# A two-layer decoder step on one core: larger interleaving steps in the attention, moved key turns, and another order at the switch to the output projection

## The chip, the cores and the metric

The kernel runs on one core of a Trainium2 chip. The metric is the device time of one execution in microseconds (us). The engines are TensorE (PE, with its weight loads as PEld), VectorE (DVE), ScalarE (ACT), GpSimd (POOL) and SyncE (SP), which issues most DMAs.

## The reference, cut to what matters

The program runs one inference step of a two-layer trunk over 1040 prompt rows (16 meta tokens and 1024 new ones) and over 8 sampled sequences of 8 new rows each. Layer 0 is a Mamba-2 mixer and a gated feed-forward. Layer 1, where the change lies, is a sliding-window attention (window 128, 16 query heads, 4 key heads of 64) and a second feed-forward:

```
q = rope((rmsnorm(h) * attn_g) @ w_q);  k, v as one shared pair from (rmsnorm(h) * kv_g)
s = q . k / 8                       # only 0 <= t - s < 128; the sampled rows also see 128 stored keys
m = max(max(s), sink[head]);  p = exp(s - m) / (sum(exp(s - m)) + exp(sink[head] - m))
h = h + (p @ v) @ w_o               # then h = h + ffn(h), and a final rmsnorm
```

All inputs are float32. A projection product is computed as three products of a high and a low part in fp32r (`mm3`: high x high, high x low, low x high). Scores, transposes and values are plain float32 products.

## The kernel before, in words

Before the stage of the change come the mixer, layer 0's feed-forward and the key and value projections (`qkv`, up to about 1793 us). Then three kinds of work are laid into one another by Python generators. Each `yield` ends a step, and `joined`/`mix` advance two generators at a given ratio. PE runs the matmuls in the order in which they were written (`in_order` over everything from `forced` on, L2331 and L2376). The order on the other engines is chosen by a planner that simulates the program, by readiness and priority.

The query projection (`queries`, called `qs`) makes 16 row blocks of 128 rows x 512 columns, eight steps each, a step being the three matmuls of one k (L73 to L75). Its result is scaled on ACT (L1963), rotated on POOL (L1778 to L1780) and turned by four transposes (L2005) inside the next block; the last block's turn stands at the end (L2023).

The prompt attention has 16 units (8 row blocks x 2 halves of the heads), class `PromptUnit`. `scores(0)` and `scores(1)` are four 64-row products each (L2073), added to a mask and reduced by DVE (L2079). `softmax` is one small and eight long exponentials on ACT (L2090, L2096), sums on DVE and two multiplications on POOL (L2099). `turn(0)` and `turn(1)` are six transposes each (L2112), copied by ACT (L2114) and, the middle part after the second, by DVE (L2119). `values` are 16 products (L2130, L2134), copied by ACT and DVE (L2137). In `prompt` the loop over x lays unit x's scores, unit x-1's softmax and unit x-2's turns and values together in five steps.

The sampled attention (`attend_sample`) has four steps for each of 8 sequences: turn the stored keys (L2160), scores (L2171, L2172) and softmax, turn the probabilities (L2185, L2186), values (L2196, L2197). SP loads the next sequence's stored keys and values, and writes 120 rows of them back, at the start of a sequence.

The three are laid together so: 24 query steps first; then 64 prompt steps (units up to x = 13) at 2 to 1 with 32 sampled steps; these 96 against the 104 query steps left. Accumulators are eight banks in four rings of two (L55): scores, turned, out (also used for the middle turn, L2107) and rows (projections).

At the switch the attention results so far are split into high and low parts (`split_copy`: ACT casts at L79, DVE subtracts at L80), all fifteen pieces at high priority (L2369). Five more attention steps run (`AHEAD`, L54), then the first half's output projection (`output_early`, 64 steps of six matmuls of 272 columns) is mixed with the remaining eleven attention steps at 4 to 5. Each projected tile is saved to DRAM by SP (L2233). Then `output_tile` projects the second half, eight tiles, each saved by SP (L2252, L1268), and layer 1's feed-forward follows.

Of the kernel before, what the change touches and what calls it, by code (L numbers as in the profile page):

```python
# [21 lines left out]
NS = 64  # L22
# [28 lines left out]
FIRST = 3  # L51
LEAD = 3
EARLY = 14
AHEAD = 5  # L54
PLACES = {"scores": ("S", 2), "turned": ("T", 2), "out": ("O", 2), "rows": ("P", 2)}  # L55

HALVES = (
# [981 lines left out]
        yield  # L1039


def mix(*args):

    for _ in joined(*args):
        pass


END = object()
# [161 lines left out]
class FeedForward:  # L1210
# [685 lines left out]
def qkv(tc, K, A, ap, fp, ps, O, I, pre):  # L1896


    nc = tc.nc
# [239 lines left out]

def attend_sample(tc, K, A, sp, ps, I, O, order):  # L2140

    nc = tc.nc
    state = []

    def load(b):
        ks, v = sp.get("kst"), sp.get("vst")
        nc.sync.dma_start(ks, I["state_k"][b].rearrange("l h d -> l (h d)"))
        nc.sync.dma_start(v, I["state_v"][b].rearrange("l h d -> l (h d)"))
        nc.sync.dma_start(O["k_s"][b, 0:120].rearrange("l h d -> l (h d)"), ks[8:])
        nc.sync.dma_start(O["v_s"][b, 0:120].rearrange("l h d -> l (h d)"), v[8:])  # L2150
        state.append((ks, v))

    load(order[0])
    for x, b in enumerate(order):
        ks, v = state.pop(0)
        if x < 7:
            load(order[x + 1])
        pk = ps.turned()
        for kv in range(NKV):
            nc.tensor.transpose(pk[:64, 128 * kv : 128 * kv + 128], ks[:, 64 * kv : 64 * kv + 64], K.ident)  # L2160
        kT = sp.get("kT", 64)
        nc.vector.tensor_copy(kT, pk[:64, :])
        q4 = sp.get("q4", 64).rearrange("p (h t) -> p h t", t=8)
        nc.gpsimd.tensor_copy(q4[:, :8], A.QS[:64, :, 8 * b : 8 * b + 8])
        nc.scalar.copy(q4[:, 8:], A.QS[64:, :, 8 * b : 8 * b + 8])
        yield
        pss = ps.scores()
        for kv in range(NKV):
            rows = slice(32 * kv, 32 * kv + 32)
            q = q4[:, 4 * kv : 4 * kv + 4].rearrange("p h t -> p (h t)")  # L2170
            nc.tensor.matmul(pss[rows, 0:128], q, kT[:, 128 * kv : 128 * kv + 128], start=True, stop=True, tile_position=(0, 32 * kv))  # L2171
            nc.tensor.matmul(pss[rows, 128:192], q, A.KS[:, kv, :], start=True, stop=True, tile_position=(0, 32 * kv))  # L2172
        P = sp.get("PD")
# [11 lines left out]
        nc.tensor.transpose(pt[:, 0:128], P[:, 0:128], K.ident)  # L2185
        nc.tensor.transpose(pt[:64, 128:256], P[:, 128:192], K.ident)  # L2186
        PT = sp.get("PTd")
        nc.vector.tensor_copy(PT[:, 0:128], pt[:, 0:128])
        nc.scalar.copy(PT[:64, 128:256], pt[:64, 128:256])
        yield  # L2190
        po = ps.turned()
        for kv in range(NKV):
            a, e = divmod(kv, 2)
            out = po[64 * e : 64 * e + 64, 32 * a : 32 * a + 32]
            vs = slice(64 * kv, 64 * kv + 64)
            nc.tensor.matmul(out, v[:, vs], PT[:, 32 * kv : 32 * kv + 32], start=True, stop=False)  # L2196
            nc.tensor.matmul(out, A.V[:NS, 0, vs], PT[:64, 128 + 32 * kv : 160 + 32 * kv], start=False, stop=True)  # L2197
        nc.scalar.copy(A.OS[:, :, 8 * b : 8 * b + 8], po[:, :64].rearrange("p (q t) -> p q t", t=8))
        yield


# [12 lines left out]
def output_early(nc, K, F, sqh, rows, oH, oL):  # L2214


    for m in range(KD):
# [5 lines left out]
        for c in range(2):  # L2223
            acc = rows()
            cs = slice(272 * c, 272 * c + 272)
            for k in range(KD):
                wH, wL = (t[:, 128 * (k % 4) : 128 * (k % 4) + 128] for t in w[k // 4])
                mm3(nc, acc[:, :272], wH, wL, oH[:, k, cs], oL[:, k, cs], k == 0, k == KD - 1)
                if k == KD - 1:
                    nc.vector.tensor_tensor(x[:, cs], x[:, cs], acc[:, :272], ALU.add)  # L2230
                    output_square(nc, K, F, sqh, x[:, cs], 0, m, 272 * c)
                    if c:
                        nc.sync.dma_start(F.saved[0][:, m], x)  # L2233
                if k % 2:
                    yield

# [18 lines left out]
def attention(tc, K, I, O, pre):  # L2255
# [6 lines left out]
    with ExitStack() as outer:  # L2262
        outer.enter_context(F.stack.pop_all())
        with ExitStack() as inner:
# [32 lines left out]
            with tp(name="qf", bufs=1) as fp:  # L2297
# [11 lines left out]
                def prompt(first, last, done=lambda u: None):  # L2309

                    n = len(units)
                    for x in range(first, last):
                        if x < n:
                            units[x].scores(0)
                            yield
                        if x >= 2:
                            units[x - 2].turn(0)
                            yield
                        if x < n:
                            units[x].scores(1)  # L2320
                            yield
                        if 0 <= x - 1 < n:
                            units[x - 1].softmax()
                        if x >= 2:
                            units[x - 2].turn(1)
                            yield
# [5 lines left out]
                for _ in range(8 * LEAD):  # L2332
# [28 lines left out]
            def split(u):  # L2361

                e, fs, o = u.i // 4, slice(4 * u.a, 4 * u.a + 4), 32 + 128 * (u.i % 4)
                split_copy(nc, OH[e][:, fs, o : o + 128], OL[e][:, fs, o : o + 128], u.O)

            with tc.high_priority(PRIO):
# [117 lines left out]
```

## Time and profile before

| | us |
|---|---|
| median of 3 runs | 2869.57 (2868.34 to 2872.6) |
| the profiled execution | 2869.85 |
| its span, first to last instruction | 2868.1 |
| PE busy | 2760.2 (96%) |
| DVE busy | 2022.5 (71%) |
| ACT busy | 1222.4 (43%) |
| POOL busy | 487.1 (17%) |

The span is what the profiler saw between the first and the last instruction; the execution's own time is 1.75 us longer. Busy shares are means over stages with different limits, so a stage is read by its own stretch. A busy PE means that a matmul is under way; at the lower of the clock's two levels (1.2 instead of 2.4 GHz) the same matmul is busy longer. The granted clock is given as a share of the higher level.

### The profile page before, as it was taken

To read this page: it belongs to the slowest core of one execution; us is meant where nothing else is said; L and a number is where in the kernel's file an instruction comes from. 1 tells how busy PE (TensorE), PEld (TensorE's weight loads), DVE (VectorE), ACT (ScalarE), POOL (GpSimd) and SP (SyncE) were. 2 spreads that over 40 slices of the span, in tenths; PEclk is the share of its full clock that TensorE was granted. 3 is DMA by queue.
4 is the path that set the end of the run, shared out by engine and by line. 5 is a ranking of instruction groups with operands and counts; after the bars stand their busy time and mean duration, and the time that the engine had idled before them with its cause. 6 is when DMAs were issued, how large, how long until landed. Compare 5 with 4: busy or idle time off the path is not lost. (4 is left out here: it accounts for less than half of the span.)

```text
span 2868.1 us, 51222 instructions
## 1 busy us (share of the span) xinstructions
PE 2760.2 (96%) x19990; PEld 2545.5 (89%) x19990; DVE 2022.5 (71%) x3633; ACT 1222.4 (43%) x2580; POOL 487.1 (17%) x692
## 2 busy tenths in 40 slices
PE   7999999899999899999999999998999999999998
PEld 7888989877888799999999997665998999999998
DVE  6779676647574698777768791555479777877786
ACT  4667554346442344333332243545434433433224
POOL 1455444314222100000000002332210000000000
PEclk9999999999999999999999999998999999999999
DMA  6776866565554434444468652001623443437664
GB/s 201 236 233 225 273 216 215 183 234 192 198 177 169 137 99 171 136 150 140 138 258 305 227 198 79 20 23 50 184 88 114 171 136 131 161 142 303 239 219 156
DMA packets 327009, 496.58 MB, mean 173 GB/s; under 512 B 24479, under 2 KB 222559, under 8 KB 325713
## 3 DMA queue, kind: packets, MB, share of 16 engines
q1 hardware_dynamic: 325614, 491.20, 50.5%
q8 instruction: 158, 2.59, 0.4%
q10 hardware_dynamic: 1152, 2.10, 0.2%
q14 instruction: 85, 0.70, 0.1%
HBM read 317.93 MB, written 175.30 MB: 172 GB/s over the span
## 5 line engine op out<-in xcount | busy, mean ns | idle before, releaser
L1149 ACT CAST wo<-ws 128x512 fp32r<-128x512 f32 x428 | 263.7, 620 | 546.1 <-PE wacc L1492 246.5
L1491 PE MATMUL dacc<-bo,wo 128*128 128x276 f32 (+1 forms) x1232 | 360.3, 292 | 10.3 <-DMA bo<-f_B 5.4
L1493 PE MATMUL dacc<-bo,wo 128*128 128x276 f32 (+1 forms) x1232 | 358.0, 291 | 0.0
L1492 PE MATMUL dacc<-bo,wo 128*128 128x276 f32 (+1 forms) x1232 | 357.9, 291 | 0.0
L1150 DVE TENSOR_TENSOR wo<-ws,wo 128x512 fp32r<-128x512 f32 x428 | 297.4, 698 | 69.0 <-ACT wo L1149 59.6
L73 PE MATMUL acc<-uH,wH 128*128 128x296 f32 (+1 forms) x840 | 276.5, 329 | 1.7 <-DVE th L762 1.6
L74 PE MATMUL acc<-uL,wH 128*128 128x296 f32 (+1 forms) x840 | 275.5, 328 | 0.0
L75 PE MATMUL acc<-uH,wL 128*128 128x296 f32 (+1 forms) x840 | 274.2, 326 | 0.9 <-DVE wL L156 0.9
L1491 PEld LDWEIGHTS dacc<-bo,wo 128*128 128x128 f32 x1232 | 234.4, 190 | 11.5 <-issue 10.9
L1492 PEld LDWEIGHTS dacc<-bo,wo 128*128 128x128 f32 x1232 | 234.4, 190 | 0.0
L1493 PEld LDWEIGHTS dacc<-bo,wo 128*128 128x128 f32 x1232 | 234.1, 190 | 0.0
L73 PEld LDWEIGHTS acc<-uH,wH 128*128 128x128 f32 x840 | 158.9, 189 | 16.7 <-issue 6.6
L75 PEld LDWEIGHTS acc<-uH,wL 128*128 128x128 f32 x840 | 158.8, 189 | 11.6 <-issue 2.3
L74 PEld LDWEIGHTS acc<-uL,wH 128*128 128x128 f32 x840 | 158.8, 189 | 10.6 <-issue 2.2
L585 DVE SCALAR_TENSOR_TENSOR cc<-raw,convw,cc 128x616 f32<-128x616 f32 (+1 forms) x144 | 134.3, 936 | 39.5 <-ACT cc L583 37.9
L1639 DVE TENSOR_TENSOR hN<-hN,dacc 128x544 f32<-128x544 f32 (+1 forms) x164 | 116.7, 720 | 27.9 <-PE dacc L1493 26.4
L73 PE MATMUL acc<-yH,wH 128*128 128x296 f32 (+1 forms) x360 | 122.3, 342 | 6.9 <-ACT yH L79 3.7
L2285 POOL MEMSET mask<- 128x64 f32 x1 | 0.2, 154 | 727.0 <-PE dacc L1493 727.0
L74 PE MATMUL acc<-yL,wH 128*128 128x296 f32 (+1 forms) x360 | 120.6, 336 | 0.1
L75 PE MATMUL acc<-yH,wL 128*128 128x296 f32 (+1 forms) x360 | 120.2, 335 | 0.0
L1491 PE MATMUL wacc<-N4H,wo 128*128 128x276 f32 (+1 forms) x352 | 102.7, 292 | 4.7 <-DVE hN L1504 2.4
L1149 ACT CAST wo<-sum 128x512 fp32r<-128x512 f32 x66 | 41.0, 622 | 154.3 <-PE wacc L1492 106.7
(594 smaller groups left out, 8615.3 us busy)
## 6 DMA issues: line engine op xcount, KB each, us to landing
kept<-wH SPq DMA_DIRECT2D x56, 512.0 KB
kept<-wL SPq DMA_DIRECT2D x56, 512.0 KB
ws<-ffn_w_gate SPq DMA_DIRECT2D x44, 512.0 KB
ws<-ffn_w_up SPq DMA_DIRECT2D x44, 512.0 KB
ws<-ffn_w_down SPq DMA_DIRECT2D x44, 512.0 KB
ws<-ssm_w_in SPq DMA_DIRECT2D x40, 512.0 KB
wH<-kept SPq DMA_DIRECT2D x38, 512.0 KB
wL<-kept SPq DMA_DIRECT2D x38, 512.0 KB
```

Source lines behind the costliest of these rows:

```text
L73: nc.tensor.matmul(out, wH, xH, start=start, stop=False)
L74: nc.tensor.matmul(out, wH, xL, start=False, stop=False)
L75: nc.tensor.matmul(out, wL, xH, start=False, stop=stop)
L585: nc.vector.scalar_tensor_tensor(o, raw[:, k : k + n], w(k), o, ALU.mult, ALU.add)
L1149: nc.scalar.copy(H, src)
L1150: (low or nc.vector).tensor_tensor(L, src, H.bitcast(F32), ALU.subtract)
L1491: nc.tensor.matmul(out, wH, xH, start=start, stop=False, skip_group_check=True)
L1492: nc.tensor.matmul(out, wH, xL, start=False, stop=False, skip_group_check=True)
L1493: nc.tensor.matmul(out, wL, xH, start=False, stop=stop, skip_group_check=True)
L1639: add = lambda d, s: nc.vector.tensor_tensor(d, d, s, ALU.add)
L2285: nc.gpsimd.memset(A.mask0[:, :NS], NEG)
```

## The change

In words: (1) A query step holds two k, six matmuls. (2) A prompt unit has three steps for five: turn(0) of unit x-2 with scores(0) of x; turn(1) of x-2 with scores(1) and the softmax of the same x; values of x-2. (3) `together` puts one sampled step directly behind each prompt step while there are any; the 40 pairs are mixed with the 52 query steps left. (4) The next sampled sequence's keys are turned between a sequence's scores and its turned probabilities; two sequences are loaded at the start, and x+2 after the values of x. (5) The sampled scores take their bank from the ring of `out` instead of `scores`. (6) The last block's queries are turned after two attention steps of the second part. (7) At the switch only the pieces that the first half's projection reads are split at high priority, in the order of need; five others follow at normal priority. (8) Two attention steps instead of five run ahead of the projection, and the mix is 2 to 5. (9) The single tiles of the projection are saved by DMAs from ACT instead of SP.

```diff
-AHEAD = 5
+AHEAD = 2
+def together(a, b):
+    for _ in a:
+        next(b, END)
+        yield
+    for _ in b:
+        pass
 # FeedForward.save
-        start = (self.nc.sync if self.layer or m is None else self.nc.scalar).dma_start
+        start = (self.nc.sync if m is None else self.nc.scalar).dma_start
 # qkv, queries
-                    yield
+                    if k % 2:
+                        yield
...
-        turned.pop(0)()
+        A.last_turn = turned.pop(0)
 # attend_sample: four functions, keys, scores, turn, values, of the same instructions
-        pss = ps.scores()
+        pss = ps.rest()
...
+    load(0)
+    load(1)
+    for x, b in enumerate(order):
+        if x == 0:
+            keys(b, S[x])
+            yield
+        scores(b, S[x])
+        yield
+        if x + 1 < len(order):
+            keys(order[x + 1], S[x + 1])
+            yield
+        turn(S[x])
+        yield
+        values(b, S[x])
+        load(x + 2)
         yield
 # output_early
-                        nc.sync.dma_start(F.saved[0][:, m], x)
+                        nc.scalar.dma_start(F.saved[0][:, m], x)
 # attention, prompt
                     for x in range(first, last):
+                        if x >= 2:
+                            units[x - 2].turn(0)
                         if x < n:
                             units[x].scores(0)
-                            yield
+                        yield
                         if x >= 2:
-                            units[x - 2].turn(0)
-                            yield
+                            units[x - 2].turn(1)
                         if x < n:
                             units[x].scores(1)
-                            yield
-                        if 0 <= x - 1 < n:
-                            units[x - 1].softmax()
+                            units[x].softmax()
+                        yield
                         if x >= 2:
-                            units[x - 2].turn(1)
-                            yield
                             units[x - 2].values()
                             done(units[x - 2])
                             yield
...
-                att = joined(prompt(0, EARLY), sample, 5 * EARLY - 6, 32)
-                mix(att, qs, 5 * EARLY - 6 + 32, 8 * (16 - LEAD))
+                att = together(prompt(0, EARLY), sample)
+                mix(att, qs, 3 * EARLY - 2, 4 * (16 - LEAD))
...
             with tc.high_priority(PRIO):
-                for e, o, a, b in ((0, 0, 40, 64), (0, 24, 32, 40), (1, 0, 0, 32)):
-                    split_copy(nc, OH[e][:, :, o : o + b - a], OL[e][:, :, o : o + b - a], A.OS[:, :, a:b])
-                for u in units[: EARLY - 2]:
-                    split(u)
+                split_sampled(0, 0, 40, 64)
+                split_sampled(0, 24, 32, 40)
+                for i in range(4):
+                    split(units[i])
+                    split(units[8 + i])
+            split_sampled(1, 0, 0, 32)
+            for i in range(4, 8):
+                split(units[i])
...
             for _ in range(AHEAD):
                 next(att)
-            mix(att, early, 4, 5)
+            A.last_turn()
+            mix(att, early, 2, 5)
```

## Rows read from the trace of the kernel before

**Rows 1.** Stretches of time: busy us of each engine (instructions), PE clock, DMA share, GB/s

```profile
1793.20:1985.20 192.00, 181.37 (x1231) 122.99 (x1229) 99.08 (x425) 94.65 (x359) 69.97 (x120) 1.00 0.11 31
1985.20:1988.10 2.90, 0.18 (x1) 0.00 (x0) 1.25 (x2) 2.62 (x8) 2.84 (x5) 1.00 0.01 3
1988.10:2008.60 20.50, 15.41 (x63) 9.73 (x64) 16.15 (x47) 12.72 (x34) 2.17 (x5) 0.50 0.17 48
2008.60:2067.70 59.10, 58.87 (x471) 54.51 (x470) 27.23 (x61) 26.13 (x64) 14.78 (x16) 1.00 0.61 175
2067.70:2119.30 51.60, 51.13 (x402) 50.41 (x401) 35.20 (x65) 17.39 (x32) 9.55 (x6) 1.00 0.54 161
2119.30:2180.00 60.70, 49.14 (x354) 47.14 (x353) 50.94 (x93) 25.07 (x44) 1.62 (x1) 0.94 0.12 36
```

**Rows 2.** Waits of PE, 1793.2 to 1985.2: us in total, times, longest

```profile
PE pO L2130 <- ACT work L2114: 4.9, 4, 1.6
PE pT L2185 <- POOL work L2182: 3.1, 4, 1.6
PE pO L2130 <- ACT work L2116: 2.3, 2, 1.4
```

**Rows 3.** PE in order of time (start, us): values that wait, and that don't

```profile
1966.51 0.65 PE L2130 MATMUL pO<-work,V 128*64 128x256 f32 x2
1968.08 1.08 PE L2130 MATMUL pO<-work,V 128*64 128x256 f32 x6 [0.92 <-ACT work L2114]
...
1969.68 0.50 PE L73 MATMUL pP<-rwH,uH 128*128 128x512 f32 x1
...
1982.82 1.08 PE L2130 MATMUL pO<-work,V 128*64 128x256 f32 x8
...
1984.42 0.50 PE L73 MATMUL pP<-rwH,uH 128*128 128x512 f32 x1
```

**Rows 4.** ACT in order of time at the first: exponentials, then the copy

```profile
1963.84 0.46 ACT L2096 ACTIVATE work<-work 128x192 f32<-128x192 f32 x1 [2.64 <-DVE work L2089]
...
1967.46 0.56 ACT L2114 COPY work<-pT 128x512 f32<-128x512 f32 x1
```

**Rows 5.** DVE by line, 1793.2 to 1985.2: busy us, mean ns, idle before

```profile
L2079 DVE CUSTOM_DVE_ANT_0 work<-pS,am_sb,sink 128x192 f32<-128x192 f32 (+1 forms) x104 | 37.6, 409 | 30.5 <-PE pS L2073 30.5
```

**Rows 6.** PE in order of time: scores, projection, transposes, projection

```profile
1976.54 0.92 PE L2073 MATMUL pS<-KT,QT 64*128 64x192 f32 x8
1977.39 0.50 PE L73 MATMUL pP<-rwH,uH 128*128 128x512 f32 x1
1977.73 0.39 PE L74 MATMUL pP<-rwL,uH 128*128 128x512 f32 x1
...
1978.20 0.27 PE L2112 MATMUL pT<-cmask_sb,work 128*128 128x128 f32 x1
...
1978.77 0.48 PE L73 MATMUL pP<-rwH,uH 128*128 128x512 f32 x1
```

**Rows 7.** Waits of PE, 1985.2 to 2068: us in total, times, longest

```profile
PE pT L2005 <- POOL qr L1780: 4.1, 1, 4.1
PE pO L2130 <- DVE work L2119: 3.3, 2, 3.1
```

**Rows 8.** POOL in order of time at the switch

```profile
1985.26 1.47 POOL L2099 TENSOR_TENSOR work<-work 128x768 f32<-128x768 f32 x1 [0.72 <-DVE work L2098]
...
1989.13 0.32 POOL L1780 TENSOR_TENSOR qr<-rt,rt 128x64 f32<-128x64 f32 x1
```

**Rows 9.** ACT in order of time at the switch: the casts of the splits

```profile
1987.94 6.34 ACT L79 CAST OH<-QT 128x512 fp32r<-128x512 f32 x12
```

**Rows 10.** SP's waits, 2030 to 2180; issues of line 1268 by ACT (ns)

```profile
SPq L1268 <- DVE hN L2250: 26.6, 7, 7.3
...
L1268 ACTq DMA_DIRECT2D res<-big x8: 326/326/338, 966.9 to 983.7; - x8
```

**Rows 11.** Waits of PE, 2068 to 2181

```profile
PE ps L1077 <- POOL tot L2211: 4.4, 1, 4.4
```

More of the change, by code (lines that the diff above doesn't have):

```diff
@@ L2142, in attend_sample @@
     nc = tc.nc
[L2143 to L2157, printed above, removed]
+    S = [Ctx() for _ in order]
@@ new lines, in load, with keys @@
+    def load(x):
+        if x >= len(order):
+            return
+        b, s = order[x], S[x]
+        s.ks, s.v = sp.get("kst"), sp.get("vst")
+        nc.sync.dma_start(s.ks, I["state_k"][b].rearrange("l h d -> l (h d)"))
+        nc.sync.dma_start(s.v, I["state_v"][b].rearrange("l h d -> l (h d)"))
+        nc.sync.dma_start(O["k_s"][b, 0:120].rearrange("l h d -> l (h d)"), s.ks[8:])
+        nc.sync.dma_start(O["v_s"][b, 0:120].rearrange("l h d -> l (h d)"), s.v[8:])
+    def keys(b, s):
@@ L2158, in attend_sample @@
         pk = ps.turned()
         for kv in range(NKV):
[L2160 to L2165, printed above, removed]
-        yield
-        pss = ps.scores()
+            nc.tensor.transpose(pk[:64, 128 * kv : 128 * kv + 128], s.ks[:, 64 * kv : 64 * kv + 64], K.ident)
@@ L2168, in attend_sample, with scores @@
+        s.kT = sp.get("kT", 64)
+        nc.vector.tensor_copy(s.kT, pk[:64, :])
+        s.q4 = sp.get("q4", 64).rearrange("p (h t) -> p h t", t=8)
+        nc.gpsimd.tensor_copy(s.q4[:, :8], A.QS[:64, :, 8 * b : 8 * b + 8])
+        nc.scalar.copy(s.q4[:, 8:], A.QS[64:, :, 8 * b : 8 * b + 8])
+    def scores(b, s):
+        pss = ps.rest()
         for kv in range(NKV):
             rows = slice(32 * kv, 32 * kv + 32)
-            q = q4[:, 4 * kv : 4 * kv + 4].rearrange("p h t -> p (h t)")
-            nc.tensor.matmul(pss[rows, 0:128], q, kT[:, 128 * kv : 128 * kv + 128], start=True, stop=True, tile_position=(0, 32 * kv))
+            q = s.q4[:, 4 * kv : 4 * kv + 4].rearrange("p h t -> p (h t)")
+            nc.tensor.matmul(pss[rows, 0:128], q, s.kT[:, 128 * kv : 128 * kv + 128], start=True, stop=True, tile_position=(0, 32 * kv))
@@ L2172, in attend_sample @@
             nc.tensor.matmul(pss[rows, 128:192], q, A.KS[:, kv, :], start=True, stop=True, tile_position=(0, 32 * kv))
-        P = sp.get("PD")
+        P = s.P = sp.get("PD")
         m, nm, es, sm = (sp.get(x) for x in ("dm", "dn", "de", "ds"))
@@ L2182, in attend_sample, with turn, values @@
         nc.gpsimd.tensor_scalar(P, P, sm, None, ALU.mult)
-        yield
+    def turn(s):
         pt = ps.turned()
[L2185 to L2189, printed above, removed]
-        yield
+        nc.tensor.transpose(pt[:, 0:128], s.P[:, 0:128], K.ident)
+        nc.tensor.transpose(pt[:64, 128:256], s.P[:, 128:192], K.ident)
+        s.PT = sp.get("PTd")
+        nc.vector.tensor_copy(s.PT[:, 0:128], pt[:, 0:128])
+        nc.scalar.copy(s.PT[:64, 128:256], pt[:64, 128:256])
+    def values(b, s):
         po = ps.turned()
@@ L2195, in attend_sample @@
             vs = slice(64 * kv, 64 * kv + 64)
-            nc.tensor.matmul(out, v[:, vs], PT[:, 32 * kv : 32 * kv + 32], start=True, stop=False)
-            nc.tensor.matmul(out, A.V[:NS, 0, vs], PT[:64, 128 + 32 * kv : 160 + 32 * kv], start=False, stop=True)
+            nc.tensor.matmul(out, s.v[:, vs], s.PT[:, 32 * kv : 32 * kv + 32], start=True, stop=False)
+            nc.tensor.matmul(out, A.V[:NS, 0, vs], s.PT[:64, 128 + 32 * kv : 160 + 32 * kv], start=False, stop=True)
         nc.scalar.copy(A.OS[:, :, 8 * b : 8 * b + 8], po[:, :64].rearrange("p (q t) -> p q t", t=8))
+    load(0)
[13 more added lines that the diff above has]
+        load(x + 2)
         yield
@@ L2312, in prompt @@
                     for x in range(first, last):
+                        if x >= 2:
+                            units[x - 2].turn(0)
                         if x < n:
                             units[x].scores(0)
-                            yield
+                        yield
                         if x >= 2:
-                            units[x - 2].turn(0)
-                            yield
+                            units[x - 2].turn(1)
                         if x < n:
                             units[x].scores(1)
-                            yield
-                        if 0 <= x - 1 < n:
-                            units[x - 1].softmax()
+                            units[x].softmax()
+                        yield
                         if x >= 2:
-                            units[x - 2].turn(1)
-                            yield
                             units[x - 2].values()
@@ L2331, in attention @@
                 forced = len(traced)
-                for _ in range(8 * LEAD):
+                for _ in range(4 * LEAD):
                     next(qs)
                 sample = attend_sample(tc, K, A, sp, ps, I, O, (4, 5, 6, 7, 0, 1, 2, 3))
-                att = joined(prompt(0, EARLY), sample, 5 * EARLY - 6, 32)
-                mix(att, qs, 5 * EARLY - 6 + 32, 8 * (16 - LEAD))
+                att = together(prompt(0, EARLY), sample)
+                mix(att, qs, 3 * EARLY - 2, 4 * (16 - LEAD))
             pre.stack.close()
@@ L2364, in split, with split_sampled @@
                 split_copy(nc, OH[e][:, fs, o : o + 128], OL[e][:, fs, o : o + 128], u.O)
+            def split_sampled(e, o, a, b):
+                split_copy(nc, OH[e][:, :, o : o + b - a], OL[e][:, :, o : o + b - a], A.OS[:, :, a:b])
             with tc.high_priority(PRIO):
-                for e, o, a, b in ((0, 0, 40, 64), (0, 24, 32, 40), (1, 0, 0, 32)):
-                    split_copy(nc, OH[e][:, :, o : o + b - a], OL[e][:, :, o : o + b - a], A.OS[:, :, a:b])
-                for u in units[: EARLY - 2]:
-                    split(u)
+                split_sampled(0, 0, 40, 64)
[6 more added lines that the diff above has]
+                split(units[i])
             early = output_early(nc, K, F, sqh, ps.rows, OH[0], OL[0])
```

## The prediction

> **What bounds the kernel now.** Read first the stages as stretches of time [rows 1]. The diff touches the fourth quarter only: the woven attention (1793.2 to 1985.2 us), the switch to the output projection (1985.2 to 2008.6), the first half's projection woven with the last attention (to 2067.7) and the second half's projection (to 2119.3). The reader is to see PE busy for 181.37 of 192.00 us, 15.6 of 23.4, 58.87 of 59.10 and 51.13 of 51.60 there, while no other engine passes 52% in the first, or 70% in any of them but the switch. PE sets the pace, so what it loses is what can be won: 10.6 us of idle in the weave, and the whole of the switch, where 20.5 us run at a granted clock of 0.50 (the 1.2 GHz level). After 2119.3 the stage that follows is DVE's (50.94 of 60.70 us); it starts when PE is done and is not shortened by the diff.
>
> Then read who PE waits for in the weave [rows 2]: the values of a prompt unit wait 4.9 + 2.3 us for ACT's copies of the turned probabilities, the sampled turn 3.1 us for POOL's multiplication: 10.3 us in ten waits. The values' wait costs more than the view lists. A values block that waits goes from 1966.51 to the next projection matmul at 1969.68, 3.17 us; one that doesn't takes 1984.42 - 1982.82 = 1.60 [rows 3]. That is 1.57 lost for 0.92 listed, 0.65 more, since two matmuls are started before the idle begins. Six times 0.65 is 3.9, so the weave loses 14.2 us. The reason stands on ACT [rows 4]: the eight exponentials of the next unit run from 1963.84 to 1967.46, 3.6 us, and the copy that the values need stands behind them.
>
> At the switch read PE's waits [rows 7], and the clock in rows 1. From 1985.2 to 2008.6 PE is busy 0.18 + 15.41 us; the 15.41 are at half clock, so they are 7.7 us of work at full clock. 23.4 - 7.9 = 15.5 us are lost there: 4.1 in the wait for the last rotated queries, 3.1 and 0.2 in the values', 7.7 in the clock, the rest in small gaps.
>
> **The change part by part.** The sum starts from the profiled execution: 2869.85 us, of which 2868.1 are span and 1.75 lie around it. The median of the runs shown is 2869.57, so nothing is corrected.
>
> *Larger steps, softmax earlier.* No matmul is added or removed. Between the second half's turn and the values there stood one or two projection steps of three matmuls; a matmul of 512 columns follows the last after 0.235 us (1977.73 to 1978.20 for two [rows 6]), so 0.7 or 1.4 us. Now there stand the second scores (0.85), a sampled piece, and one or two steps of six (1.4 or 2.8): at least 2.25 us, against a copy of 0.56 us [rows 4]. And the exponentials of that step can't begin before it, since they need four reductions of 0.41 us, 1.6 us, after scores that come behind the turn [rows 5]. The six waits of the values go: -11.1 us (7.2 + 3.9).
>
> *Keys between scores and turned probabilities.* A whole step with its projection matmuls now stands between a sampled sequence's scores and its turn, 4 us or so instead of 0.7 to 1.4. The waits were 3.1 us in four, 1.6 at most, so they go: -3.1. The loads: still 32 state transfers on SP; two sequences at the start, then each behind the values two sequences before it. SP waits for PE there as it did before, and what is queued behind it is the w_o tiles, which nothing needs before 1985. The new keys are wanted two steps, some 8 us, after their load is issued: no cost.
>
> *Sampled scores in the ring of two that holds the middle turn and the values.* Twice in eight their step falls directly behind a unit's values, whose first copy is on ACT, now behind that unit's exponentials. Exponentials end 1.6 + 3.6 = 5.2 us after the second scores, the copy (0.4, a half of the 0.56 row and its overhead) at 5.6; the values end 2.65 + 1.60 = 4.25 after them at the earliest. So 1.3 us each, 2.6 in all. Bounds: 0 if the copy goes first, 2 x (3.6 + 0.4) = 8 if all exponentials are still ahead. I take 2.6, since ACT is busy for 49% of the stage.
>
> *Fewer changes between kinds.* Scores after projection: 0.85 us, and the next projection matmul then takes 0.34 instead of 0.235, so about 0.1 on the way out and as much on the way in; a block of transposes takes 0.57 for six, and costs nothing around it [rows 6]. Sixteen sampled blocks (scores and values) now lie behind a prompt block: bounds 0 and 16 x 0.2 = -3.2; I take -1, as most of the blocks beside them are transposes. The Trainium skill says in "TensorEngine Tiling (Array Packing)", Key Properties, that "Mode switching requires drain"; the 0.1 us on each side of the 64-row scores agrees, and by that rule alone, since the sampled pieces use other tilings than the prompt's, nothing would be saved here and the gain would be 1 us smaller.
>
> The weave then: -11.1 - 3.1 + 2.6 - 1 = -12.6.
>
> *The last query turn behind two attention steps, splits by need.* POOL ends the last rotation 4.2 us after PE's last projection matmul: 1.5 us of a softmax multiplication are ahead of it [rows 8]. Now two attention steps stand in between: two half turns and two scores, 2 x (0.57 + 1.05) = 3.2 us. 1 us of the 4.1 remains; but the softmax of unit 13 now also comes at the end and POOL has its two multiplications of 1.47 to do: bounds 0 and 4.1, taken 1.5. ACT then: 12 casts took 6.34 us, 0.53 each [rows 9]; at high priority are now ten (two sampled, eight units) instead of fifteen, 5.3 us, ahead of the two copies that the values of unit 12 need. With 1.1 us before them these are ready 7.5 us after the last projection, where PE arrives after 3.2 + 0.4 + 1.5 = 5.1: 2.4 us of wait; bounds 0 (copies first) and 6 (DVE's ten subtractions also ahead). The first projection of the output finds w_o and its splits 0 to 2 us late; 0.6 taken. So 4.5 us lost in place of 15.5: -11.0. The five splits set back cost ACT and DVE 3 us each, in a stretch where they are busy 26.13 and 27.23 of 59.10 us [rows 1].
>
> The clock: in the weave waits of 1.6 us left it at 1.00 [rows 1, 2], the 4.1 us wait was followed by 20.5 us at 0.50 [rows 1, 7]. My waits of 1.5 and 2.4 are nearer to the first, so nothing is taken; the bound is the 7.7 us again.
>
> *Steps at 2 to 5 instead of 4 to 5, two ahead instead of five.* The ten attention steps left use 25 of the projection's 64 steps, where eleven used 14. The second half's residual is loaded when the attention ends, and 39 steps are still to come: nothing. Two or three steps of six short matmuls between attention steps cover the copies: nothing either.
>
> *Sixteen saves from SP to ACT.* Issuing one on ACT took 0.33 us [rows 10], 5.3 in all where ACT has more than half its time free; the square before each has waited for the same data, so ACT waits no longer. SP loses waits of 26.6 us behind which weight loads stood [rows 10]. PE's 4.4 us wait at the end of the projection [rows 11] follows a DVE queue that had waited for such a load. Bounds +4 (ACT late with a cast) and -8 (this wait and half of the idle after 2119.3 gone); I take -2.
>
> Sum: -12.6 - 11.0 - 2.0 = -25.6; 2869.85 - 25.6 = 2844.
>
> **The rivals.**
> 1. *The switch stays as it was.* Ten casts at high priority, the POOL chain and the merged steps leave one wait of 3 us or more, and the clock falls again. For it: both engines are in order, and the 3.1 us wait on DVE [rows 7] came from such splits. Against: five fewer, and no wait of 4.1 before them. Only the weave and the saves are won: 2869.85 - 14.6 = 2855. The Trainium skill's "TensorE: Matmul & The Clock Gate" (HAM oscillation) warns of just this, bursts between waits that are each started at half clock; the 20.5 us at 0.50 behind a 4.1 us wait agree.
> 2. *The loads were the hidden bound of what follows.* Without the saves SP runs ahead, DVE's sums move forward, and 8 us of the 11.6 us of PE's idle time in 2119.3 to 2180 go, not 2: 2844 - 6 = 2838, and lower with a better switch.
> 3. *The gain is absorbed.* PE is earlier, but the stage after 2119.3 waits for DVE, which gets its splits later and its loads no sooner. Half the gain goes there: 2857 to 2868, say 2862. Against it: DVE is busy only 35.20 of 51.60 us before.
> 4. *Slower.* The ring of two: all copies of a unit's values stand behind its own eight exponentials, issued one step earlier, and the next unit's middle turn waits for them. My margin is thin: copy done at 5.6 us, buffer wanted at 4.25 + 0.2 + 1.4 = 5.85 after the second scores. If DVE's reductions start 2 us late, each of twelve units waits about 2; from 2.1 us a unit (25.6 / 12) nothing is left, and with the full 3.6 + 0.4 us each it is 12 x 4 = 48 lost: 2844 + 48 - 2.6 = 2889. Against it: DVE is busy for 52% of the stage only.
>
> **How the numbers follow.** 0.2% of the time is 5.7 us, about what a measurement of this kernel can tell from no change. The forecast has a chance of 0.56, rival 1 0.16, rival 2 0.11, rival 3 0.10, rival 4 0.07. Faster holds the forecast, rivals 1 and 2 and a part of 3: 0.87; within 0.2% the rest of 3: 0.06; slower 0.07. The bounds of the forecast's own terms add to -12 and +15; rivals 1 and 3 lie inside the upper one or just above, so the range is 2827 to 2864.
>
> **What would show it.** In the changed profile: values no longer wait for the turned copies, and no sampled turn waits for POOL; the weave takes 179 us from its first scores to the last query projection; scores of sampled sequences wait twice, for ACT. The first projection of the output begins about 10 us after the last query projection, not 21.8, with the clock at 1.00 or at 0.50 for a few us only. SP issues no saves there. Wrong it would be if values waited once in every unit, now for the ring's copies; if the clock stood at 0.50 for 20 us again; or if the stage after the projection grew by what the weave lost.

## The result, and the profile after

The changed kernel takes 2850.12 us, median of 6 runs (2845.12 to 2854.42); the kernel before 2869.27 in the same runs (6, 2868.29 to 2872.71). The ratio is 0.993, interval 0.9917 to 0.9943: 19 us or 0.7% faster. Forecast were 2844 and faster; the time is 6 us above the forecast and inside the range. The profiled execution of the changed kernel is its longest, 2854.42 us with a span of 2852.6. So the pair of traces differs by 15.5 us, not by 19; what follows accounts for the 15.5.

The stages of the changed kernel first, as stretches of time, in the columns of [rows 1]: the weave from its first scores to the last query projection, the switch to the first projection of the output, the first half's projection, the second half's, and what follows.

```profile
1795.90:1983.60 187.70, 176.77 (x1231) 129.06 (x1231) 93.45 (x423) 92.85 (x357) 68.81 (x120) 0.96 0.11 32
1983.60:1990.50 6.90, 6.03 (x49) 3.73 (x47) 5.85 (x24) 6.75 (x18) 4.19 (x9) 1.00 0.08 12
1990.50:2056.30 65.80, 62.49 (x489) 57.62 (x486) 39.33 (x90) 34.66 (x91) 16.69 (x16) 0.97 0.64 186
2056.30:2107.70 51.40, 51.40 (x408) 51.03 (x408) 40.78 (x71) 19.52 (x35) 10.88 (x7) 1.00 0.50 148
2107.70:2168.40 60.70, 53.59 (x402) 51.74 (x402) 51.52 (x95) 25.09 (x44) 0.00 (x0) 0.97 0.16 46
```

Cut by the same instructions, the stages stand like this (us):

| | weave | to the first output projection | first half | second half | what follows |
|---|---|---|---|---|---|
| before | 191.7 | 21.6 | 60.8 | 56.9 | 743.4 |
| after | 187.7 | 6.9 | 65.8 | 51.4 | 744.9 |

What lies ahead of the weave is 2.2 us longer in this execution and what follows the second half 1.5; no edit touches either, and such differences stand between most of the profiles below. The weave gives 4.0 us where 12.6 were forecast, switch and first half together 9.7 (11.0 forecast), the second half 5.5 (2.0).

Why the weave gives so little is seen in PE's waits there, answering to [rows 2]:

```profile
PE pT L2196 <- POOL work L2192: 9.8, 4, 3.3
PE pO L2181 <- DVE QT L2147: 1.1, 2, 0.6
```

The values' waits are gone. But the sampled turn, which should no longer have waited, waits 9.8 us for POOL in place of 3.1, and its longest waits are followed by half clock: the granted clock of the stage is 0.96, not 1.00. Half clock at the longest wait but one, as a stretch of time:

```profile
1942.50:1949.30 6.80, 5.61 (x15) 4.32 (x16) 0.29 (x1) 1.10 (x3) 2.34 (x7) 0.50 0.01 2
```

Follow that wait through three engines, each in order of time. PE issues the last sequence's scores behind the prompt's, and later waits for the turn:

```profile
1933.78 0.92 PE L2083 MATMUL pS<-KT,QT 64*128 64x192 f32 x8
1934.63 0.44 PE L2181 MATMUL pO<-work 64*32 64x128 f32 x8
...
1943.69 0.47 PE L2196 MATMUL pT<-cmask_sb,work 128*128 128x128 f32 x1 [3.17 <-POOL work L2192]
...
1944.60 0.63 PE L74 MATMUL pP<-rwL,uH 128*128 128x512 f32 x1
```

ACT does the prompt's eight exponentials (line 2106) first, and then the sampled one (line 2188):

```profile
1936.62 0.46 ACT L2106 ACTIVATE work<-work 128x192 f32<-128x192 f32 x1 [2.05 <-DVE work L2099]
...
1939.81 0.44 ACT L2106 ACTIVATE work<-work 128x192 f32<-128x192 f32 x1
...
1940.24 0.44 ACT L2188 ACTIVATE work<-work 128x192 f32<-128x192 f32 x1
```

POOL does the prompt's second multiplication (line 2109), and then the sampled one:

```profile
1941.43 1.47 POOL L2109 TENSOR_TENSOR work<-work 128x768 f32<-128x768 f32 x1 [0.76 <-DVE work L2190]
1942.87 0.76 POOL L2192 TENSOR_SCALAR work<-work 128x192 f32<-128x192 f32 x1
```

The sampled chain ends 9.0 us after its scores began (1943.63 - 1934.63). Over the eight sequences it took 3.7 to 7.2 us before the change; now it takes 8.1, 9.4, 4.6, 12.2, 8.6, 3.7, 4.6 and 9.0. The four that wait are the first, fourth, fifth and eighth. The first, fifth and eighth have their scores in the same step as the prompt's second scores and softmax. So has the second, whose turn comes late enough (10.2) to hide it; the fourth is another case, seen in the fifth run.

### The profile page after: what moved, and what is told of

Same layout as the page of the kernel before. It is cut to its first block, busy times and chain, and to the rows that moved or that the text cites. A ratio compares the mean times of both kernels' runs of the same rounds, so it can differ in the third digit from the quotient of the medians.

```text
span 2852.6 us, 51198 instructions
## 1 busy us (share of the span) xinstructions
PE 2751.4 (96%) x19990; PEld 2550.4 (89%) x19990; DVE 2015.6 (71%) x3633; ACT 1220.3 (43%) x2580; POOL 487.9 (17%) x692
## 4 chain that ended last, share of the span: by engine, by line
PE 81%; DVE 6%; ACT 2%; issue 1%; DMA 1%; POOL 1%; SPq 0%; DVEq 0%; ACTq 0%; POOLq 0%
PE wacc L1500 10%; PE wacc L1502 10%; PE wacc L1501 10%; PE acc L74 6%; PE acc L73 6%; PE acc L75 6%; PE dacc L1500 6%; PE dacc L1501 5%; PE dacc L1502 5%; PE pP L73 2%; PE pP L75 2%; PE pP L74 2%; PE ps L670 1%; PE ps L667 1%; PE pS L2083 1%
```

## The experiments

Each ran beside the kernel before, and the ratio is to that. "Weave" is the stage of the table above in its profile; "turn" is PE's wait for the sampled multiplication in it.

| | median us | ratio (interval) | weave | turn |
|---|---|---|---|---|
| after | 2850.12 | 0.993 (0.9917 to 0.9943) | 187.7 | 9.8 |
| 1 multiplication on DVE | 2844.34 | 0.9913 (0.99 to 0.9925) | 183.5 | 7.0 |
| 2 saves back on SP | 2854.59 | 0.995 (0.9938 to 0.9962) | 184.0 | 9.8 |
| 3 before, saves on ACT | 2863.88 | 0.998 (0.997 to 0.9989) | 191.7 | 3.1 |
| 4 the weave alone | 2863.35 | 0.9979 (0.9971 to 0.9988) | 187.7 | 9.8 |
| 5 chain set ahead | 2843.26 | 0.991 (0.9894 to 0.9926) | 179.5 | 5.8 |
| 6 and a last step | 2837.79 | 0.989 (0.9875 to 0.9905) | 178.0 | 4.3 |
| 7 splits in the old order | 2851.89 | 0.9934 (0.9916 to 0.9952) | 186.3 | 10.0 |
| 8 last turn first | 2856.86 | 0.9955 (0.9939 to 0.9972) | 185.8 | 9.8 |
| 9 pairs swapped | 2848.81 | 0.993 (0.9917 to 0.9942) | 184.4 | 0.7 |
| 10 two steps of room | 2834.05 | 0.9879 (0.9865 to 0.9894) | 174.7 | 1.9 |
| 11 both of 5 and 10 | 2835.23 | 0.9885 (0.9867 to 0.9903) | 173.6 | 0.8 |
| 12 10, projection in small steps | 2839.01 | 0.9888 (0.987 to 0.9907) | 173.5 | 1.6 |

The weave of one profile is not exact to a few us. The changed kernel and runs 2, 4, 7 and 8 have the same weave with the same four waits of the turn, and it takes 184.0 to 187.7 us, because the half clock stands over 6.8 to 13.7 us of it; the changed kernel's profile is at the long end. The wait of 3.25 us before 1869.50 is followed by a stretch at 0.50 from 1870.8 in the changed kernel. In run 2 the same wait is followed by the full clock, by PE in order of time and the stretch behind it:

```profile
1868.78 0.33 PE L2196 MATMUL pT<-cmask_sb,work 128*128 128x128 f32 x1 [3.25 <-POOL work L2192]
```

```profile
1868.80:1875.60 6.80, 6.80 (x45) 5.48 (x46) 2.43 (x11) 1.97 (x9) 3.10 (x3) 1.00 0.08 24
```

**1. The sampled multiplication on DVE.**

```
-        nc.gpsimd.tensor_scalar(P, P, sm, None, ALU.mult)
+        nc.vector.tensor_scalar(P, P, sm, None, ALU.mult)
```

> The changed kernel with one edit: the sampled softmax's last multiplication runs on DVE instead of POOL. Theory A: the weave won 4.0 us of the 12.6 forecast because this multiplication stands behind the prompt softmax's two multiplications in POOL's in-order queue, so that the sampled turn waits (9.8 us in four, by the changed kernel's trace) and each longer wait is followed by half clock. Then the waits of the sampled turn fall under 2 us, the clock stays at 1.00 in the weave, the weave takes 171 to 177 us (187.5 now) and the time is 2834 to 2841. Rival B: the chain of the sampled softmax itself is too long, whoever multiplies; the waits stay above 6 us, now for DVE, and the time is within 4 us of the changed kernel's 2850.

Measured: 2844.34, between the two. PE waits for DVE in place of POOL:

```profile
PE pT L2196 <- DVE work L2192: 7.0, 4, 2.5
```

So POOL's queue is the smaller part, and what lies ahead of the multiplication the larger. Part of the gain is lost in a way that nobody had counted. DVE's multiplication takes 0.32 us with POOL idle, and 1.24 to 1.47 in the four sequences where POOL runs the prompt's at the same time; DVE and POOL at the last of them, in order of time:

```profile
1935.36 1.47 DVE L2192 TENSOR_SCALAR work<-work 128x192 f32<-128x192 f32 x1
```

```profile
1935.25 1.47 POOL L2109 TENSOR_TENSOR work<-work 128x768 f32<-128x768 f32 x1 [0.76 <-DVE work L2190]
```

In all four DVE's ends 0.11 to 0.12 us after POOL's. The Trainium skill says in "SBUF — State Buffer" (SBUF: two separate sides) of the port pair that the two engines share: "The shared pair is an **exclusive lock**, not a bandwidth split"; the four ends agree with it.

**2 and 3. The saves.** The second run undoes two lines of the change, the third makes them alone in the kernel before:

```
-        start = (self.nc.sync if m is None else self.nc.scalar).dma_start
+        start = (self.nc.sync if self.layer or m is None else self.nc.scalar).dma_start
...
-                        nc.scalar.dma_start(F.saved[0][:, m], x)
+                        nc.sync.dma_start(F.saved[0][:, m], x)
```

> The changed kernel with the sixteen saves back on SP. Theory C: the second half's projection became 5.4 us shorter (56.2 to 50.8) because the saves left SP, so that the loads behind them come sooner and DVE isn't held up before the last tiles. Then the 4 us wait of PE for the sums of squares comes back and the time is 4 to 6 us above the changed kernel: 2854 to 2857. Rival D: the shorter stage comes from the other order of splits and of work on DVE; then the time is within 2 us of 2850 and the wait stays away.

> The kernel before with only the sixteen saves moved from SP to ACT. Theory C: the second half's projection loses its 4.4 us wait, the time is 2863 to 2866. Rival D: the wait stays, 2868 to 2871. A third case: ACT issues hold up its casts, 2871 to 2874.

Measured: 4.5 us lost by the one (its interval touches the changed kernel's), 5.5 won by the other. PE's wait of [rows 11] is back in the run that undoes it, and has no row in the third:

```profile
PE ps L1086 <- POOL tot L2239: 4.2, 1, 4.2
```

**4. The weave alone**: steps, sampled order and ring as changed; the last query turn, the splits and the saves as before; one whole unit (three of the larger steps) runs ahead of the projection and the rest is mixed at 2 to 3.

> The changed kernel's weave alone: larger steps, earlier softmax, keys moved, sampled scores in the ring of the values; the saves on SP, the last query turn directly behind the queries, all fifteen pieces split at high priority, one whole unit ahead of the projection and the rest mixed at 2 to 3, as before in kind. If the stages add up, the weave gives 4.0 us, the switch nothing and the second half nothing: 2864 to 2867. If part of the switch's gain comes from the weave's order (softmax of the last woven unit ended earlier, fewer pieces of the attention left), the switch is 3 to 6 us shorter too: 2858 to 2862.

Measured: 6.0 us won, its weave 4.0 shorter in the profile, as in the changed kernel: the turn's 9.8 us are the weave's own. At the switch the wait for the last query rows is there as in [rows 7], 5.2 us of it.

**5 and 6. The sampled chain set ahead.** The lines from the maximum to the multiplication stand under a higher priority; the sixth run also gives the last sequence a step before its turn.

```
+        with tc.high_priority(PRIO):
             P = s.P = sp.get("PD")
             ...
             nc.gpsimd.tensor_scalar(P, P, sm, None, ALU.mult)
...
         if x + 1 < len(order):
             keys(order[x + 1], S[x + 1])
-            yield
+        yield
```

> The changed kernel with the sampled sequence's softmax chain set ahead of other work by the planner's priority: its exponential then stands behind four instead of eight exponentials of the prompt on ACT, nothing else moves. Theory A (ACT's order, not POOL alone, makes the sampled turn late): the turn's waits fall from 17 us (for POOL or DVE) to under 8 us and the time by 4 to 12 us, 2838 to 2846. Rival (the weave loses by something that stands elsewhere, the sampled turns only show it): within 3 us of the changed kernel, with the waits moved to the prompt's turns, whose exponentials come later by one sampled exponential.

> As the run before, and the last sampled sequence also gets a step of its own between its scores and its turned probabilities, as the others have by the next sequence's keys. Theory A: the last sequence's turn waits no longer, 1 to 2 us less than the run before. Rival: one more step only shifts the work behind it, no difference.

Measured: 2843.26 and 2837.79. The wait falls from 9.8 us (not from the 17 that the expectation names) to 5.8 and 4.3, and does not move to the prompt's turns, which have no row. In the fifth run the exponential stands behind five of the prompt's long ones, not four, and starts 3.8 to 4.3 us after the scores, not 5.0 to 5.6, in the four sequences beside a softmax. The fourth sequence, which is none of these, still waits 3.2. There the chain stands among the rounding of the second half's query weights, which has high priority too and itself waits for PE; ACT of that run in order of time:

```profile
1859.53 0.73 ACT L1808 ACTIVATE rwH<-QT,gains 128x512 fp32r<-128x512 f32 x1 [1.46 <-PE pP L75]
1860.16 0.44 ACT L2189 ACTIVATE work<-work 128x192 f32<-128x192 f32 x1
```

The two runs' intervals overlap, so what the last step alone brings is open; its wait went.

**7. The splits at the switch in their old order**, sampled sequences first, then the units by number, and all fifteen at high priority again.

> The changed kernel with the splits at the switch in their old order (sampled sequences first, then the prompt's units by number). Theory (the order by need shortens the switch): the first output projection starts 2 to 4 us later, the time is 2852 to 2855. Rival (the switch gained by the weights, the last query turn and the saves, not by the splits): within 1.5 us of 2850.

Measured: 2851.89, inside the interval of the changed kernel. Neither the order by need nor the lower priority of five is worth anything that these runs can tell, though the first projection does wait longer, by this row of PE's waits at the switch against 2.2 us in one wait in the changed kernel:

```profile
PE pP L74 <- DVE OL L80: 4.3, 2, 2.3
```

**8. The last query turn directly behind the queries.**

```
-        A.last_turn = turned.pop(0)
+        turned.pop(0)()
...
-            A.last_turn()
```

> The changed kernel with the last query turn directly behind the queries, as before. Theory (the moved turn fills the wait at the switch): the turn waits 4 to 5 us for its rows instead of 0.7 us, the clock falls to the lower of its two levels for the stretch behind it, together 6 to 12 us more, 2856 to 2862. Rival (the wait was lost time that the switch has anyway, behind the casts): within 3 us of 2850.

Measured: 2856.86, 6.7 more than the changed kernel; the interval of the ratio touches its. From the last query projection to the first of the output 16.4 us pass in place of 6.9. PE's waits there, and that stretch of time:

```profile
PE pT L2014 <- POOL qr L1789: 5.2, 1, 5.2
```

```profile
1979.80:1996.20 16.40, 9.55 (x49) 5.89 (x48) 12.40 (x29) 12.30 (x28) 4.77 (x9) 0.69 0.06 18
```

**9. The steps of each pair swapped**, the sampled one issued first.

```
-    for _ in a:
-        next(b, END)
+    for _ in b:
+        next(a, END)
         yield
-    for _ in b:
-        pass
+    for _ in a:
+        yield
```

> The changed kernel with the two steps of each pair swapped: the sampled sequence's step is issued ahead of the prompt's, so that its exponential, sums and multiplication stand ahead of the prompt's softmax of the same pair on ACT, DVE and POOL. Theory A (the sampled chain is late because it is queued behind the prompt's softmax of its own pair): the sampled turns wait under 5 us in all, the time is 2838 to 2846. Rival (the order of the pair doesn't matter, since the next pair's prompt work is ahead of the multiplication then): sampled turns wait as long as before the swap, within 3 us of 2850.

Measured: 2848.81, no gain, though the turn waits 0.7 us only. That is neither case as written: the mechanism goes as theory A has it, the time doesn't. PE waits elsewhere now:

```profile
PE pT L2122 <- DVE QT L2015: 2.9, 2, 2.3
PE pT L2209 <- ACT work L2200: 1.6, 1, 1.6
```

Its two waits of over 1.5 us stand ten microseconds apart, and a stretch at half clock follows each:

```profile
1860.90:1881.50 20.60, 18.96 (x112) 13.81 (x112) 8.43 (x34) 8.07 (x28) 4.87 (x9) 0.75 0.05 16
```

A quarter of 20.6 us is 5.1 lost. Against the tenth run its weave is 9.7 us longer: 2.3 by waits, 5.1 by the clock, and 2.3 that stay open.

**10 and 11. Two steps of room.** The values of the sequence before move between the scores and the next keys; keys and values are loaded by themselves for that. The eleventh run adds the priority of the fifth.

```
...
     for x, b in enumerate(order):
         scores(b, S[x])
         yield
+        if x:
+            values(order[x - 1], S[x - 1])
+            load_values(x + 1)
+            yield
         if x + 1 < len(order):
             keys(order[x + 1], S[x + 1])
+            load_keys(x + 3)
             yield
         turn(S[x])
         yield
-        values(b, S[x])
-        load(x + 2)
-        yield
+    values(order[-1], S[-1])
+    yield
```

> The changed kernel with two steps in place of one between a sampled sequence's scores and its turned probabilities: the values of the sequence before stand there beside the next sequence's keys (keys and values of the state are loaded by themselves for it, with the same lead). Nothing is set ahead in any queue. Theory A (one step is shorter than the chain of 7 to 12 us, two are longer): the sampled turns wait only in the first sequence and the last, under 5 us in all, and the stretch behind them keeps the full clock; the time is 2836 to 2844. Rival B (the lost time comes from the queues as such, and the chain grows with the room it is given): waits of 8 us or more stay, within 3 us of 2850.

> The run before, with the sampled chain also set ahead by the planner's priority. Theory A: nearly nothing is left to gain, 0 to 2 us under the run before. Rival B: the priority brings the 7 us again that it brought without the two steps, 2840 to 2843 where the run before stays at 2850.

Measured: 2834.05, 35 us under the kernel before and 16 under the changed one (the intervals lie apart), and 2835.23, the same. The tenth run's weave as a stretch of time, and PE's waits in it:

```profile
1791.90:1966.50 174.60, 170.86 (x1231) 124.86 (x1231) 93.82 (x423) 92.97 (x357) 68.54 (x120) 1.00 0.12 34
```

```profile
PE pT L2202 <- POOL work L2198: 1.9, 1, 1.9
PE pO L2187 <- DVE QT L2147: 1.3, 2, 0.8
PE pO L2187 <- ACT QT L2147: 0.5, 1, 0.5
```

The same 1231 instructions keep PE busy 170.86 us at a clock of 1.00 and 176.77 at 0.96. So the half clock cost the changed kernel's profile 5.9 us beside the waits that it follows; that is near half of the 12.4 us that PE was busy there at 0.50. In run 2, with the same waits, PE was busy at 0.50 for 4.4 us of the weave. The tenth run is the fastest of all and beats both kernels.

**12. The projection in small steps.** The tenth run, with the query projection's step of one slice again.

> The run with two steps between sampled scores and turn, with the projection's steps of half the size again: one slice of three matmuls, not two, between two steps of attention, as before the change (so 104 changes from attention to a projection matmul in the weave in place of 52). Theory A (the projection's first matmul takes 90 ns more behind another kind, 484 ns on average before and 437 after for 104 of them): their mean goes back to 480 to 487 ns, the weave is 4.5 to 6 us longer than 174.7, the time is 2838 to 2841. Rival (the mean fell by the order of the attention steps, not by the size of the projection's): 437 ns stays and the time is within 2 us of 2834.

Measured: 2839.01, 5 us more by the medians and 2.6 by the ratios, with an interval that overlaps the tenth's. The weave has no part in it, 173.5 us; in the profiles what lies ahead of the weave is 3.6 us longer, where no edit touches, the first half's projection 2.1 and what follows the second 1.8. The mean of the projection's first matmuls, by line, in the tenth run and in this one:

```profile
L73 PE MATMUL pP<-rwH,u 128*128 128x512 f32 x40 | 17.5, 437 | 0.0
L73 PE MATMUL pP<-rwH,uH 128*128 128x512 f32 x32 | 14.0, 436 | 0.0
L73 PE MATMUL pP<-rwH,bo 128*128 128x512 f32 x32 | 13.7, 427 | 0.0
```

```profile
L73 PE MATMUL pP<-rwH,u 128*128 128x512 f32 x40 | 17.6, 439 | 0.0
L73 PE MATMUL pP<-rwH,bo 128*128 128x512 f32 x32 | 14.0, 437 | 0.0
L73 PE MATMUL pP<-rwH,uH 128*128 128x512 f32 x32 | 14.0, 437 | 0.0
```

My theory fell. A projection matmul follows another kind 48 times here and 43 in the tenth run, so the size of the projection's step hardly matters: 40 steps of attention go in among it either way, where before there were 96.

## Why the prediction was right, and where it failed

That the time came out only 6 us above the forecast is in part luck, as errors of opposite sign cancel. In the profiles the turn (+9.8 us against the forecast) and the clock (+5.9) cost 15.7 that the sum did not have; the changes between kinds (5.4), the saves (3.5) and the ring (1.5) gave 10.4 more than it had. The range, too, is narrower than the sum behind it: the bounds given for the single terms add to -15 and +28, and not to -12 and +15 (ring -2.6 and +5.4, changes -2.2 and +1, switch -4.5 and +7.6, clock +7.7, saves -6 and +6).

**The sampled turn, the step that failed** ("the waits were 3.1 us in four, 1.6 at most, so they go: -3.1"). They grew by 6.7. The working gave the chain a longer way on PE, and took for granted that it stays as long as before. The same edit puts the prompt's softmax into the step ahead of the sampled scores, so that eight exponentials stand before it on ACT and multiplications of 1.47 us on POOL. Their 3.6 us stood in [rows 4]; I used them for the values alone. That is the case of three of the four waits. The fourth sequence's 3.25 us have another cause, the rounding of the query weights among which its chain stands (run 5). The runs that set the chain ahead or give it room take away waits and time: the tenth 7.9 us of the turn's waits and 5.9 of the clock's, with a weave 13.0 shorter and 16 us in the median.

**The clock in the weave** (taken as nothing). Three of the four waits, of 1.9 to 3.3 us, were followed by stretches at 0.50, and the one of 1.5 us was not: 5.9 us by the tenth run. In [rows 2] waits of 1.6 us had left it at 1.00, and that was no bound for waits of 3. Nor does the length of a wait decide it here: the fourth sequence's wait of 3.2 to 3.5 us stands in seven profiles (the changed kernel, runs 2 and 4 to 8), with half clock behind it in five of them and the full clock in runs 2 and 5.

**The values' waits** (-11.1) were right: the listed 7.2 us are gone, and their first matmuls keep PE busy 13.0 us in place of 16.8, so 11.0 with the part that the view of waits doesn't list. PE by line, in the weave before (busy and mean, idle before it) and after:

```profile
L2130 PE MATMUL pO<-work,V 128*64 128x256 f32 (+1 forms) x96 | 16.8, 395 | 7.2 <-ACT work L2114 4.9 <-ACT work L2116 2.3
...
L73 PE MATMUL pP<-rwH,u 128*128 128x512 f32 x40 | 19.3, 482 | 0.0
L73 PE MATMUL pP<-rwH,bo 128*128 128x512 f32 x32 | 15.6, 487 | 0.0
L73 PE MATMUL pP<-rwH,uH 128*128 128x512 f32 x32 | 15.4, 483 | 0.0
```

```profile
L2140 PE MATMUL pO<-work,V 128*64 128x256 f32 (+1 forms) x96 | 13.0, 392 | 0.0
```

**Fewer changes between kinds** (-1, bound -3.2) was mis-sized: the price was right and the count was not. Take PE in order of time, from one matmul's start to the next. A projection matmul between others of its kind takes 0.23 us; the last one ahead of scores or values takes 0.33, and the first one behind them 0.34. That is the 0.1 us on each side of the forecast. This row stands just ahead of the scores at 1976.54 in [rows 6]:

```profile
1976.22 0.39 PE L75 MATMUL pP<-rwH,bo 128*128 128x512 f32 x1
```

Behind transposes nothing is lost: the first projection matmul starts 0.03 us after the last transpose and takes 0.32 to the next start, together about what a transpose (0.11) and a projection matmul (0.23) take anyway. The term looked at the sampled blocks alone. But a projection matmul follows another kind 97 times before and 43 in the tenth run, and of these scores or values 56 and 24 times. Summed from start to start, without the waits, the projection's matmuls take 9.3 us less in the tenth run than before, the prompt's scores 1.4 less, and the transposes 4.1 more, since 25 blocks of them now have scores behind them, at 0.20 in place of 0.11, and fewer a projection matmul at 0.03. With 0.2 of small terms that makes -6.4. The Trainium skill's "Mode switching requires drain" ("TensorEngine Tiling (Array Packing)", Key Properties) agrees at the scores and values, whose tilings are other than the projection's; at the sampled turn's transposes of 128x64, which change the tiling too, this trace shows no price. By that rule alone I had the gain smaller, where counting the changes by it makes it larger.

**The sampled scores in the ring of two** (+2.6) were seen as forecast, two waits directly behind the values, but for DVE's copy and 1.1 us.

The weave adds up: -11.0 (values), -6.4 (changes of kind), +6.7 (turn), +1.1 (ring) and +5.9 (clock) make -3.7, measured -4.0. Without turn and clock it would have been as in the tenth run, 17 us shorter.

**The switch** (-11.0; measured 9.7 with the first half) was right in sum, and three of its parts less so. PE's waits from the last query projection to the end of the first half, answering to [rows 7]:

```profile
PE pP L74 <- DVE OL L80: 2.2, 1, 2.2
PE pS L2083 <- DVE work L2089: 0.8, 1, 0.8
PE pT L2014 <- POOL qr L1789: 0.7, 1, 0.7
PE pO L2122 <- DVE QT L2147: 0.3, 1, 0.3
```

The last turn waits 0.7 us (1.5 forecast) and the values not at all (2.4): their copies on ACT stand ahead of all casts, and not behind ten. The price is paid by the first projection, 2.2 us in place of 0.6, and it waits for DVE. ACT's casts for it begin at 1986.97 (the prompt's at 1987.37), but DVE first reduces scores and splits two tiles of w_o, and starts the subtractions of the splits (line 80) at 1990.22 only. ACT and DVE in order of time:

```profile
1985.97 0.58 ACT L2124 COPY work<-pT 128x512 f32<-128x512 f32 x1
...
1986.97 0.50 ACT L79 CAST OH<-OS 128x192 fp32r<-128x192 f32 x2
1987.37 4.26 ACT L79 CAST OH<-QT 128x512 fp32r<-128x512 f32 x8
```

```profile
1989.62 0.68 DVE L2015 COPY QT<-pT 128x512 f32<-128x512 f32 x1
1990.22 0.48 DVE L80 TENSOR_TENSOR OL<-OS,OH 128x192 fp32r<-128x192 f32 x2
...
1992.31 3.69 DVE L80 TENSOR_TENSOR OL<-QT,OH 128x512 fp32r<-128x512 f32 x6
```

And 3.4 us behind the first projection's wait run at half clock, 1.7 of them lost, by this stretch of time:

```profile
1993.70:1997.10 3.40, 3.40 (x17) 3.40 (x17) 3.40 (x7) 3.40 (x15) 0.00 (x0) 0.50 0.00 0
```

So the switch loses 5.7 us, where 4.5 were forecast. Of this the moved turn is the part that the eighth run shows; the splits' order shows nothing in the seventh. Two steps ahead in place of five, and the mix of 2 to 5, were not run by themselves.

**The saves** (-2) were taken too small: the whole wait of [rows 11] went, 4.5 and 5.5 us by two runs. That it hangs on the saves I had from the queue's waits in [rows 10], and then took half for want of a proof. ACT issues the saves at 326 ns, the price that [rows 10] gave. The wait is not gone for good: in seven of the runs in which ACT issues the saves (1, 5, 7 and 9 to 12) 0.8 to 2.8 us of it are back, 1.5 in the tenth by this row of its waits. What it hangs on there is open.

```profile
PE ps L1086 <- POOL tot L2250: 1.5, 1, 1.5
```

Of the rivals, the switch as it was, the gain absorbed later and the slower case show nowhere; what follows the second half is 1.5 us longer. The hidden loads are half borne out: the 4.4 us wait went, and no more of the idle time around it. The runs give -6.0 (weave), -5.5 (saves), -6.7 (last turn): 18 of the 19 us.

## What to carry to other kernels

A step that is moved can lengthen the chains that it now stands in front of, on each engine that they pass: take the time of the chain in its new place, not the wait of the old one. Where a short chain of one stream and a long softmax of another share engines, give the short chain a step more of room rather than a place ahead in the queues; here that was worth 16 us, twice the priority's 7. And a wait of 2 or 3 us on PE can cost more than itself, as the clock may fall behind it; it did so in some executions and not in others, so one profile does not price it.

## What the runs showed of the hardware that was not expected

A DVE multiplication of 128x192 in fp32 took 0.32 us with POOL idle (twice in two) and 1.24 to 1.47 beside POOL's multiplication of 128x768 or 128x576, four times in four. A projection matmul of 512 columns takes 0.1 us more on the side of scores or values (0.33 and 0.34 us to the next start against 0.23), and nothing more beside transposes. A wait of PE of 3.2 to 3.5 us, the same in seven profiles, was followed by half clock in five and by the full clock in two; in the ninth run one of 1.6 us was followed by 6.8 us at 0.50.
